# Output-projection weights emitted with the last score row, their low parts on VectorE, a new PSUM pool order, and a closing addition on two engines

## The chip, the core and the metric

The kernel runs on one core of one Trainium2 chip. The metric is the device time of one execution in microseconds (us). Five engines work side by side, each through its own list of instructions in a fixed order: TensorE (PE: matmuls, with its weight loads shown as PEld), VectorE (DVE), ScalarE (ACT), GpSimd (POOL) and SyncE (SP), which here only issues DMA transfers. An engine whose next instruction must wait holds back all that is queued behind it.

## The reference

One encoder layer on x of 1024 frames by 1024 features, in float32:

```python
u = rms_norm(h, mix_norm_gain)
proj = u @ w_in
aq, ak, av, dqkv, dgate, da, db = jnp.split(proj, SPLITS, axis=-1)
...
o_att = rms_norm(chunked_rel_attention(aq, ak, av, ...), att_out_gain)   # 8 heads of 64, band of 9 chunks
...
o_dn = rms_norm(gated_delta_rule(dq, dk, dv, log_decay, beta), dn_out_gain) * silu(dgate)  # 4 heads of 128
mixed = jnp.concatenate([o_att, o_dn], axis=-1) @ w_out
h = h + mixed
z = rms_norm(h, ffn_norm_gain) @ w_ff1
h = h + jnp.square(jax.nn.relu(z)) @ w_ff2
```

## The kernel before

Each product of full precision is made of three matmuls. `split` (L202 to L204) takes a float32 tile apart: ScalarE casts it to a high part `_h` (L203), and another engine subtracts that from the tile to get the low part `_l` (L204). `mm3` (L217 to L223; its matmul is L222) then adds hi·hi, hi·lo and lo·hi into one PSUM bank. A weight block goes through `load_w` (L208): SP issues its load into a raw tile `_r` (L210), of which the pool "wr" has three slots, ScalarE makes the high part, and the low part goes in turn to GpSimd and VectorE (`lo_turn`, L213). A fourth load can be issued only when the first block's low part is done and its slot free.

The program has these stages, in order of time: the input projections; the two mixers, attention and delta rule, woven together (to about 545 us); the output projection with `w_out` (547 to 648); the first feed-forward product `ff1` (649 to 960); the second, `ff2` (to 1266); and the last stores. Both feed-forward products use a scheme of seven block products p1 to p7 (one Strassen-like step), so that additions on VectorE feed TensorE; they keep PSUM tiles of two banks from a pool `psw` of four, tag "bk" (L1327, L1415).

`attention` (L829 to L1184) is a planner. It keeps a model clock, and in each turn emits the cheapest ready step: a score unit, a transpose ("flip"), a product with the values, a delta-rule step, and, once all flips are out and the delta rule has come to its last steps (L1124), a step of the generator `outputs()`, which is `out_proj` (L1186). What is emitted early gets an early place in the engines' lists, which a scheduler then settles by its own estimates.

`out_proj` computes, transposed, 512 columns by 512 frames at a time: `weights(0)` loads the eight 128x512 blocks of the first column half of `w_out` in the order 4, 5, 6, 7, 0, 1, 2, 3; `mixed(0)` splits the mixers' results for the first 512 frames (`mh`, `ml`; blocks 4 to 7 are the delta rule's, tile `mixd`, 0 to 3 attention's, tile `mixa`); `rows(0, 0)` makes four PSUM banks `op` of 24 matmuls each; then `weights(1)`, `rows(1, 0)`, `mixed(1)`, `rows(1, 1)`, `rows(0, 1)`. After each bank VectorE adds the residual x (`h`, L1223). Names used below: `wo_k_r`, `wo_k_h`, `wo_k_l` are the raw, high and low tiles of block k of `w_out`. `c_att`, `c_po`, `c_o` belong to the last delta-rule step, `t_tpa`, `t_tpb`, `t_ta`, `t_tb`, `t_on`, `t_o` to the last attention tile (transposes on TensorE, copies out of PSUM, the product with the values). `wa` are the first weights of `ff1` (L1315), two loads of 512 KB. On GpSimd the rsqrt chains of the normalisations run (`t_v`, `c_v`, L187 to L199).

PSUM has eight banks. The mixers' pools take them in the order of their allocation: `ps_a` three (L132), `ps_t` two, `ps_o` one, `ps_d` two. The banks `op` come from `ps_a`. `ff1`'s first tile of two banks lies where the mixers' first two banks lay.

At the end of `ff2`, with kb the last, partial sums y1 to y7 are merged and stored: `merge(nc.gpsimd, 5, 7)` (L1558) adds y7 to y5 in two halves of 128x1024 on GpSimd, whose stores ScalarE's queue issues (L1464); product p4 is then subtracted from y4 in four quarters on VectorE (L1566), each stored by SP (L1567).

Of the kernel before, what the change touches and what calls it, by code (L numbers as in the profile page):

```python
# [11 lines left out]
ALU = mybir.AluOpType  # L12
AX = mybir.AxisListType

P = 128
SEQ = 1024
DM = 1024
NKT = DM // P
# [25 lines left out]
NV = 6  # L44
# [54 lines left out]
def hymba_kernel(  # L99
# [20 lines left out]
    nc = tc.nc  # L120
    PS = bass.MemoryType.PSUM
# [4 lines left out]
    mixer = ctx.enter_context(ExitStack())  # L126
# [2 lines left out]
    pools = {tag: mixer.enter_context(tc.tile_pool(name="pool_" + tag, bufs=n)) for tag, n in slots.items()}  # L129
    spool = mixer.enter_context(tc.tile_pool(name="spool", bufs=12))  # L130
    mpool = mixer.enter_context(tc.tile_pool(name="mpool", bufs=1))
    ps_a = mixer.enter_context(tc.tile_pool(name="ps_a", bufs=3, space=PS))  # L132
    ps_t = mixer.enter_context(tc.tile_pool(name="ps_t", bufs=2, space=PS))
    ps_o = mixer.enter_context(tc.tile_pool(name="ps_o", bufs=1, space=PS))
    ps_d = mixer.enter_context(tc.tile_pool(name="ps_d", bufs=2, space=PS))

    def page(tag, name, dt=F32, w=512):
        return pools[tag].tile([P, w], dt, tag=tag, name=name, bufs=slots[tag])
# [8 lines left out]
    def part(t, i):  # L147
        return t[:, i * 512:(i + 1) * 512]
# [53 lines left out]
    def split(src, hi, lo, hi_eng, lo_eng):  # L202
        a = nc.scalar.copy(hi, src) if hi_eng is nc.scalar else hi_eng.tensor_copy(hi, src)  # L203
        return a.ins, lo_eng.tensor_tensor(lo, src, hi.bitcast(F32), ALU.subtract).ins  # L204

    lo_turn = [0]

    def load_w(src, name, tags=("wh", "wl")):  # L208
        raw = page("wr", name + "_r")
        nc.sync.dma_start(out=raw, in_=src)  # L210
        hi = page(tags[0], name + "_h", F32R)
        lo = page(tags[1], name + "_l", F32R)
        lo_turn[0] += 1  # L213
        split(raw, hi, lo, nc.scalar, nc.gpsimd if lo_turn[0] % 2 else nc.vector)
        return hi, lo

    def mm3(ps, terms, first=True, last=True):  # L217
        n = 3 * len(terms)
        i = 0
        for (ah, al), (bh, bl) in terms:  # L220
# [8 lines left out]
    u = [[(page("u", f"uh{hf}_{k}", F32R), part(u_low[k // 4], k % 4) if hf else page("u", f"ul{hf}_{k}", F32R))  # L229
          for k in range(NKT)] for hf in range(2)]  # L230
# [580 lines left out]
    def delta_all(ab, kTs, W):  # L811

        Ys, D = {}, {}
        yield dict(M=chained(delta_merge(0, W, Ys), delta_merge(1, W, Ys)))
        for c in range(NT + LATE):
            gens = {}
            if c < NT:
                gens["S"] = delta_state(c, ab, kTs, Ys, D)
            if 0 < c <= NT:
                gens["O"] = delta_out(c - 1, ab, kTs, D)  # L820
            if c + 2 < NT:
                gens["M"] = delta_merge(c + 2, W, Ys)
                if c == 2:
                    gens["M"] = chained(delta_low(1, W, "wh"), gens["M"])
            if c >= LATE:
                gens["F"] = delta_fin(c - LATE, D)
            yield gens

    def attention(after, delta, values, outputs):  # L829


        def bias_page(tag, name):
# [239 lines left out]
        units = [(g, t, pp) for g in range(2) for t in range(NT) for pp in range(2)]  # L1072
        size = [min(t + 1, 5) for g, t, pp in units]
        total, spent, deltas, begun, multiplied = sum(size), 0, 0, 0, 0
# [22 lines left out]
        while True:  # L1097
# [36 lines left out]
            k = best[2]  # L1134
            if k in live:
                gen = live[k][0]
                before = clock.now
                want = next(gen, None)
                deltas += clock.now - before
                if want is None:  # L1140
                    del live[k]
                else:
                    live[k] = gen, want
            elif k == "multiply":
                multiply(*units[multiplied][0:2])
                pe(2 * 218 * size[multiplied] + 300)
                spent += 2 * size[multiplied]
                t = give("o", on("s", 366, clock.now + LATENCY, ahead=True))
                later.append((t, finish, units[multiplied][0:2]))
                multiplied += 2  # L1150
            elif k == "later":
                _, step, args = later.pop(0)
                step(*args)
                if step is finish:
                    t = give("t", on("v", 420, pe(220), ahead=True))
                    if args[0]:
                        t = on("v", 853, on("g", 3200, on("s", 780, t)))
                        later.append((t + MARGIN, turn, args[1:]))
                        later.sort(key=lambda p: p[0])
                else:  # L1160
                    give("t", on("v", 682, pe(440), ahead=True))
            elif k == "flip":
                want = next(flipping[0], None)
                flipping = want and (flipping[0], want)
                if want is None:
                    flipped += 1
            elif k == "score":
                g, t, pp = units[begun]
                score(g, t, pp)
                begun += 1  # L1170
                if pp and begun + 2 < len(units):
                    start(*units[begun + 2][0:2])
                if pp and not g:
                    load_rest(t + 1)
            elif k == "values":
                if next(values, None) is None:
                    values_left = False
                else:
                    give("a", on("s", 690, pe(5500)))
            else:  # L1180
                next(outputs_gen)
                pe(690)
                fill += 1
        return outputs_gen or outputs()  # L1184

    def out_proj(result):  # L1186


        order = (4, 5, 6, 7, 0, 1, 2, 3)
        w, parts, R, begun = [], [], {}, []  # L1190

        def weights(j):
            w.append([None] * NKT)
            for k in order:
                w[j][k] = load_w(w_out[k * P:(k + 1) * P, j * 512:(j + 1) * 512], f"wo{j}_{k}",
                                 (("wh", "u"), ("u", "wl"))[j])

        def mixed(hf):
            parts.append([None] * NKT)
# [33 lines left out]
                nc.scalar.mul(part(r, i), part(r, i), fgain[:, 4 * j + i:4 * j + i + 1])  # L1233
            return acc

        weights(0)
        mixed(0)
        acc = yield from rows(0, 0, None)
        weights(1)
        acc = yield from rows(1, 0, acc)  # L1240
        nc.sync.dma_start(out=sq_dr[:, 0:TH], in_=acc)
        mixed(1)
# [172 lines left out]
    def ff2(psw, pools):  # L1415

        NK = 4
        y = {i: quarter(f"y{i}") for i in (1, 2, 3, 4, 5, 6)}
# [5 lines left out]
        y = {i: [wide(t, 0), wide(t, 1)] for i, t in y.items()}  # L1424
# [43 lines left out]
        for kb in range(nb):  # L1468
# [40 lines left out]
            def merge(eng, i, z):  # L1509
                for m in range(2):  # L1510
                    eng.tensor_tensor(y[i][m], y[i][m], y[z][m], ALU.add)  # L1511
# [43 lines left out]
            if last:  # L1555
                merge(nc.vector, 7, 6)
                merge(nc.vector, 4, 7)
                merge(nc.gpsimd, 5, 7)  # L1558
                store(y[5], 1, 1, nc.scalar)
            ps = product(f"p4{kb}", prep4, last)  # L1560
            if not last:
# [31 lines left out]
    kT = []  # L1593
# [8 lines left out]
    for _ in delta_proj(u, DK, 4, "dk", None, kT, w_dk, first):  # L1602
        pass
    ab = ab_proj(u)
    W, result = [], {}
    after = []
    values = att_proj(u, AV, "v", after)
    interleave(
# [1 line left out]
                 att_proj(u, AK, "k"), att_proj(u, AQ, "q"), first_steps(values, NV)), 1.0),  # L1610
        (chained(delta_prep(kT, ab), (1000 for _ in delta_low(0, W, "pp"))), 0.35))
    clock.reset()
    rest = attention(after[NV - 1], delta_all(ab, kT, W), values, lambda: out_proj(result))
    for _ in rest or ():
        pass
    mixer.close()
# [50 lines left out]
```

## Time and profile before

| what | before |
|---|---|
| time, median of 3 runs | 1276.42 us (1275.62 to 1279.3) |
| the profiled execution's own time | 1273.11 us |
| its span | 1271.0 us |
| mean granted TensorE clock | 0.995 |
| PE busy / PEld busy | 1241.2 us (98%) / 1033.3 us (81%) |
| DVE busy / ACT busy / POOL busy | 926.5 (73%) / 547.6 (43%) / 289.8 us (23%) |

The profile is one execution; its own time is 2.1 us above its span, and lies 3.3 us below the median of the runs. In a row of a timeline stand the start, the duration, the engine, the line, what is written from what, how many instructions ("x3"), and in brackets how long the engine stood idle before them and on what it waited. In a row of the windows each engine's busy time in that stretch is followed by its number of instructions; the figures at the end are the granted TensorE clock (1.00 is full speed), the mean busy share of the DMA engines and GB/s.

### The profile page before, as it was taken

The numbers are of one execution on the slowest core, as the hardware profiler recorded it, in microseconds if no ns is written. First come the engines' busy times: TensorE is split into PE (matmuls) and PEld (weight loads), VectorE is DVE, ScalarE is ACT, GpSimd is POOL, SyncE is SP. The second block draws the span as 40 slices with busy tenths as digits, with TensorE's granted clock in tenths as the row PEclk, the third lists the DMA queues.
The fourth block names the chain that finished last, engine by engine and source line by source line (L and its number), as shares of the span: only waits on it lengthen the run. The fifth ranks groups of instructions, "written<-read, shape, count | busy, mean of one in ns | idle before, by whom it ended". The sixth has DMA issues, their size and how long they took to land.

```text
span 1271.0 us, 18018 instructions
## 1 busy us (share of the span) xinstructions
PE 1241.2 (98%) x6686; PEld 1033.3 (81%) x6686; DVE 926.5 (73%) x1388; ACT 547.6 (43%) x899; POOL 289.8 (23%) x487
## 2 busy tenths in 40 slices
PE   9999999999998999889999999999999999999998
PEld 8778878778888898778878788888887888888886
DVE  7899987654236577774349777677669997997988
ACT  7323132232245665654445454544445543333331
POOL 4425461344132345543210000000000000000034
PEclk9999999999999999989999999999999999999999
DMA  7214353564585532134441333332259623332002
GB/s 226 67 42 139 101 157 107 121 162 118 175 245 150 162 109 71 40 109 133 141 141 67 116 133 117 132 100 96 86 199 368 211 83 112 121 100 94 7 34 99
DMA packets 135398, 158.53 MB, mean 125 GB/s; under 512 B 31760, under 2 KB 79376, under 8 KB 134800
## 3 DMA queue, kind: packets, MB, share of 16 engines
q1 hardware_dynamic: 117216, 135.11, 35.0%
q10 hardware_dynamic: 18096, 22.29, 5.2%
q8 instruction: 52, 0.85, 0.3%
q14 instruction: 34, 0.28, 0.1%
HBM read 109.91 MB, written 47.45 MB: 124 GB/s over the span
## 4 chain that ended last, share of the span: by engine, by line
PE 51%; DVE 8%; issue 2%; ACT 1%; POOLq 1%; POOL 0%; DVEq 0%; ACTq 0%
PE p L1439 21%; PE q L1343 20%; PE op L222 6%; PE t_o L1024 1%; POOLq L1662 1%; DVE ml L204 1%; DVE h L1285 1%; DVE y L1511 0%; PE t_sa L925 0%; DVE q_0a_l L204 0%; DVE y L1507 0%; PE t_tpb L985 0%; DVE p43b_l L204 0%; DVE p73b_l L204 0%; DVE p43a_l L204 0%
## 5 line engine op out<-in xcount | busy, mean ns | idle before, releaser
L1511 POOL TENSOR_TENSOR y<-y,y 128x1024 f32<-128x1024 f32 x6 | 19.3, 3242 | 590.5 <-DVE y L1507 571.6
L1507 DVE TENSOR_TENSOR y<-y,p 128x1024 f32<-128x1024 f32 x46 | 55.1, 1216 | 5.4 <-PE p L1439 4.5
L222 PE MATMUL op<-mh,wo_l 128*128 128x512 f32 x128 | 50.1, 399 | 1.1 <-POOL wo_l L204 1.1
L222 PE MATMUL op<-mh,wo_h 128*128 128x512 f32 x128 | 50.6, 398 | 0.1
L222 PE MATMUL op<-ml,wo_h 128*128 128x512 f32 x128 | 50.2, 395 | 0.0
L945 DVE CUSTOM_DVE_ANT_0 t_pb<-t_sb,biasn 128x256 f32<-128x256 f32 (+1 forms) x64 | 23.2, 401 | 29.8 <-PE t_sb L925 29.8
L964 ACT ACTIVATE t_pb<-t_pb,t_nm 128x256 f32<-128x256 f32 (+1 forms) x64 | 31.4, 491 | 18.1 <-DVE t_nm L956 16.7
L1223 DVE TENSOR_TENSOR h<-op,op_x 128x512 f32<-128x512 f32 x16 | 10.8, 687 | 28.8 <-PE op L222 28.8
L1230 POOL TENSOR_TENSOR op_q<-op_q 128x512 f32<-128x512 f32 x14 | 19.6, 1397 | 47.3 <-ACT op_q L1229 47.2
L222 PEld LDWEIGHTS op<-mh,wo_l 128*128 128x128 f32 x128 | 24.4, 191 | 6.9 <-POOL wo_l L204 1.5
L222 PEld LDWEIGHTS op<-mh,wo_h 128*128 128x128 f32 x128 | 24.4, 191 | 5.9 <-issue 0.5
L222 PEld LDWEIGHTS op<-ml,wo_h 128*128 128x128 f32 x128 | 24.4, 190 | 5.2
L956 DVE CUSTOM_DVE_ANT_0 t_pa<-t_sa,biaso,t_nm 128x384 f32<-128x384 f32 (+2 forms) x48 | 25.0, 543 | 2.3 <-PE t_sa L925 2.0
L222 PE MATMUL g_ps<-uh,wg_h 128*128 128x512 f32 x64 | 25.3, 396 | 1.2 <-ACT wg_h L203 1.2
L968 ACT ACTIVATE t_pa<-t_pa,t_nm 128x384 f32<-128x384 f32 (+2 forms) x48 | 26.4, 550 | 0.0
L222 PE MATMUL aq_ps<-waq_h,uh 128*128 128x512 f32 x64 | 25.4, 400 | 0.8 <-ACT waq_h L203 0.8
L925 PE MATMUL t_sb<-ks,t_q 128*128 128x256 f32 (+1 forms) x144 | 24.0, 294 | 1.7 <-DVE t_nm L945 1.3
L222 PE MATMUL g_ps<-uh,wg_l 128*128 128x512 f32 x64 | 25.2, 393 | 0.4 <-POOL wg_l L204 0.4
L222 PE MATMUL dq_ps<-uh,wdq_h 128*128 128x512 f32 x64 | 25.5, 398 | 0.0
L222 PE MATMUL dv_ps<-uh,wdv_l 128*128 128x512 f32 x64 | 25.4, 397 | 0.0
L222 PE MATMUL dq_ps<-ul,wdq_h 128*128 128x512 f32 x64 | 25.3, 395 | 0.0
L222 PE MATMUL av_ps<-wav_l,uh 128*128 128x512 f32 x64 | 25.2, 394 | 0.0
(1109 smaller groups left out, 4306.7 us busy)
## 6 DMA issues: line engine op xcount, KB each, us to landing
wa<-in_w_ff_dram SPq DMA_DIRECT2D x32, 512.0 KB
a<-in_w_ff_dram SPq DMA_DIRECT2D x32, 512.0 KB
b<-f_dr SPq DMA_DIRECT2D x32, 512.0 KB
f_dr<-yy ACTq DMA_DIRECT2D x16, 512.0 KB
t_q<-q_dr SPq DMA_DIRECT2D x30, 256.0 KB
f_dr<-zz ACTq DMA_DIRECT2D x13, 512.0 KB
ks<-k_dr SPq DMA_DIRECT2D x16, 256.0 KB
wo_r<-in_w_out_dram SPq DMA_DIRECT2D x16, 256.0 KB
```

The source lines that it names most:

```text
L204: return a.ins, lo_eng.tensor_tensor(lo, src, hi.bitcast(F32), ALU.subtract).ins
L222: nc.tensor.matmul(ps, a, b, start=(first and i == 0), stop=(last and i == n - 1))
L925: nc.tensor.matmul(o, q[m][:, i * P:(i + 1) * P], k[:, c], start=(m == 0), stop=(m == 1))
L945: nc.vector.tensor_tensor_reduce(sb[:, c], bk[:, c], new[g][pp][:, c], -1.0, 3.0e38, ALU.add, ALU.min, nm[:, 4 + i:5 + i])
L956: nc.vector.tensor_tensor_reduce(sa[e][:, 0:wa], bk[:, 0:wa], old[g][i][:, 384 - wa:384], -1.0, nm[:, 4 + i:5 + i], ALU.add, ALU.min, nm[: ...
L964: nc.scalar.activation(sb[:, c], sb[:, c], AF.Exp, bias=m, scale=-1.0, accum_out=T["sums"][:, 4 + i:5 + i])
L968: nc.scalar.activation(sa[e][:, 0:wa], sa[e][:, 0:wa], AF.Exp, bias=m, scale=-1.0, accum_out=T["sums"][:, i:i + 1])
L1230: nc.gpsimd.tensor_tensor(acc, acc, sq, ALU.add)
L1343: nc.tensor.matmul(part(ps, q), l[:, s], r, start=(k + m == 0), stop=(k == 3 and m == 2))
L1439: nc.tensor.matmul(part(ps[q], 0) if by_rows else part(ps[q // 2], q % 2), l[:, s], part(r, k), start=(i + k + m == 0), stop=(i + k + m == 4))
L1507: nc.vector.tensor_tensor(y[i][m], y[i][m], ps[m], op)
L1511: eng.tensor_tensor(y[i][m], y[i][m], y[z][m], ALU.add)
```

## The change

Four things are changed.

1. `weights(0)` becomes `out_weights(w, 0)` and is no longer the first thing in `out_proj`: the planner emits it, at high priority, as soon as it has emitted the last score unit. `out_weights(w, 1)` stays between `rows(0, 0)` and `rows(1, 0)`.
2. The low parts of all sixteen blocks of `w_out` go to VectorE; half of them were on GpSimd.
3. `ps_a` is allocated last of the mixers' PSUM pools, so its three banks are the last three, and the first two belong to `ps_t`.
4. The closing y5 += y7 is shared: its first half stays on GpSimd, its second goes to VectorE.

```diff
-    ps_a = mixer.enter_context(tc.tile_pool(name="ps_a", bufs=3, space=PS))
     ps_t = mixer.enter_context(tc.tile_pool(name="ps_t", bufs=2, space=PS))
     ps_o = mixer.enter_context(tc.tile_pool(name="ps_o", bufs=1, space=PS))
     ps_d = mixer.enter_context(tc.tile_pool(name="ps_d", bufs=2, space=PS))
+    ps_a = mixer.enter_context(tc.tile_pool(name="ps_a", bufs=3, space=PS))
...
-    def load_w(src, name, tags=("wh", "wl")):
+    def load_w(src, name, tags=("wh", "wl"), low=None):
...
-        split(raw, hi, lo, nc.scalar, nc.gpsimd if lo_turn[0] % 2 else nc.vector)
+        split(raw, hi, lo, nc.scalar, low or (nc.gpsimd if lo_turn[0] % 2 else nc.vector))
...
-    def attention(after, delta, values, outputs):
+    def attention(after, delta, values, weights, outputs):
...
                 begun += 1
+                if begun == len(units):
+                    with tc.high_priority():
+                        weights()
...
-    def out_proj(result):
...
+    def out_weights(w, j):
+        w.append([None] * NKT)
+        for k in order:
+            w[j][k] = load_w(w_out[k * P:(k + 1) * P, j * 512:(j + 1) * 512], f"wo{j}_{k}",
+                             (("wh", "u"), ("u", "wl"))[j], nc.vector)
...
-        weights(0)
         mixed(0)
         acc = yield from rows(0, 0, None)
-        weights(1)
+        out_weights(w, 1)
...
-                merge(nc.gpsimd, 5, 7)
+                for m, eng in enumerate((nc.gpsimd, nc.vector)):
+                    eng.tensor_tensor(y[5][m], y[5][m], y[7][m], ALU.add)
```

**VectorE where the output projection begins.** These rows follow the last score's maximum (L956) on VectorE, first before the change.

```order
L807 SCALAR_TENSOR_TENSOR mixd_6009<-c_tpo,dng,c_jg 128x4x128
L780 TENSOR_TENSOR c_att<-c_mt,c_Lt 128x512
L1051 TENSOR_TENSOR t_on<-t_on,t_tot 128x256
L204 TENSOR_TENSOR ml_6651<-mixd_4680,mh_6650 128x512
L786 TENSOR_TENSOR c_o<-c_o,c_po 128x512
L204 TENSOR_TENSOR ml_6655<-mixd_4680,mh_6654 128x512
```

The same place after the change:

```order
L204 TENSOR_TENSOR wo_4_l<-wo_4_r,wo_4_h 128x512
L204 TENSOR_TENSOR wo_5_l<-wo_5_r,wo_5_h 128x512
L204 TENSOR_TENSOR wo_6_l<-wo_6_r,wo_6_h 128x512
L807 SCALAR_TENSOR_TENSOR mixd_6009<-c_tpo,dng,c_jg 128x4x128
L780 TENSOR_TENSOR c_att<-c_mt,c_Lt 128x512
L1051 TENSOR_TENSOR t_on<-t_on,t_tot 128x256
L204 TENSOR_TENSOR ml_6651<-mixd_4680,mh_6650 128x512
```

Three low parts stand ahead of `c_att`; before, `wo_5_l` stood fifteen rows further down, and `wo_4_l` and `wo_6_l` were on GpSimd, behind both rsqrt chains and between `c_v` and `c_y`.

**ScalarE at the same place**, from the last exponential of the scores (L968) on, before the change:

```order
L968 ACTIVATE t_pa_6422,t_sum<-t_pa_6422,t_nm 128x384
L203 CAST mh_6650<-mixd_4680 128x512
L203 CAST mh_6654<-mixd_4680 128x512
L1006 COPY t_ta_6519<-t_tpa_6515 128x384
L203 CAST mh_6666<-mixa_5563 128x512
L203 CAST mh_6670<-mixa_5563 128x512
L203 CAST mh_6658<-mixd_4680 128x512
L1056 ACTIVATE t_on,t_oss<-t_on 128x512
L203 CAST mh_6662<-mixd_4680 128x512
```

And after the change:

```order
L968 ACTIVATE t_pa_6422,t_sum<-t_pa_6422,t_nm 128x384
L203 CAST mh_6650<-mixd_4680 128x512
L203 CAST mh_6654<-mixd_4680 128x512
L203 CAST mh_6658<-mixd_4680 128x512
L1056 ACTIVATE t_on,t_oss<-t_on 128x512
L203 CAST wo_7_h<-wo_7_r 128x512
L203 CAST mh_6662<-mixd_4680 128x512
L203 CAST wo_0_h<-wo_0_r 128x512
L203 CAST wo_1_h<-wo_1_r 128x512
L541 ACTIVATE c_po<-c_o 128x512
L203 CAST wo_2_h<-wo_2_r 128x512
L203 CAST wo_3_h<-wo_3_r 128x512
```

The five casts of the blocks that are loaded late, `wo_7_h` to `wo_3_h`, moved up from behind the attention tile's last copy; that tile's copy `t_ta` (L1006) now follows `wo_3_h`, and the casts of `mixa` follow the copies.

**VectorE at the end of the program**, before the change:

```order
L1511 TENSOR_TENSOR y_9457<-y_9457,y_0_9460 128x1024
L1511 TENSOR_TENSOR y_9457<-y_9457,y_1_9461 128x1024
L1566 TENSOR_TENSOR y_9457<-y_9457,p_11528 128x512
L1566 TENSOR_TENSOR y_9457<-y_9457,p_11529 128x512
L1566 TENSOR_TENSOR y_9457<-y_9457,p_11530 128x512
L1566 TENSOR_TENSOR y_9457<-y_9457,p_11531 128x512
```

And after it (lines below the added ones are four or five higher):

```order
L1514 TENSOR_TENSOR y_9457<-y_9457,y_0_9460 128x1024
L1514 TENSOR_TENSOR y_9457<-y_9457,y_1_9461 128x1024
L1562 TENSOR_TENSOR y_9458<-y_9458,y_1_9461 128x1024
L1570 TENSOR_TENSOR y_9457<-y_9457,p_11528 128x512
L1570 TENSOR_TENSOR y_9457<-y_9457,p_11529 128x512
L1570 TENSOR_TENSOR y_9457<-y_9457,p_11530 128x512
L1570 TENSOR_TENSOR y_9457<-y_9457,p_11531 128x512
```

The shared addition's second half (L1562) stands ahead of the four subtractions (L1570) that free the last stores.

On SP the three loads `wo_4_r`, `wo_5_r` and `wo_6_r`, which stood behind the delta rule's loads `l_w` (L630) and `m_sa` (L665), now stand among the `l_w` loads, 7, 7 and 2 rows earlier; the other five stand where they stood, right behind the two loads `wa`.

More of the change, by code (lines that the diff above doesn't have):

```diff
@@ L1184, in attention, with out_proj @@
         return outputs_gen or outputs()
-    def out_proj(result):
[L1189 to L1196, printed above, removed]
+    order = (4, 5, 6, 7, 0, 1, 2, 3)
+    def out_weights(w, j):
[3 more added lines that the diff above has]
+                             (("wh", "u"), ("u", "wl"))[j], nc.vector)
+    def out_proj(result, w):
+        parts, R, begun = [], {}, []
         def mixed(hf):
@@ L1604, in hymba_kernel @@
     ab = ab_proj(u)
-    W, result = [], {}
+    W, w_o, result = [], [], {}
     after = []
@@ L1612, in hymba_kernel @@
     clock.reset()
-    rest = attention(after[NV - 1], delta_all(ab, kT, W), values, lambda: out_proj(result))
+    rest = attention(after[NV - 1], delta_all(ab, kT, W), values,
+                     lambda: out_weights(w_o, 0), lambda: out_proj(result, w_o))
     for _ in rest or ():
```

## The prediction

> **What bounds the kernel now.** I read the page first: the span, the busy line, and the chain that ended last.
>
> ```profile
> span 1271.0 us, 18018 instructions
> PE 1241.2 (98%) x6686; PEld 1033.3 (81%) x6686; DVE 926.5 (73%) x1388; ACT 547.6 (43%) x899; POOL 289.8 (23%) x487
> PE 51%; DVE 8%; issue 2%; ACT 1%; POOLq 1%; POOL 0%; DVEq 0%; ACTq 0%
> ```
>
> PE is busy in all but 30 us of the span, so time can only come out of PE's idle spots, or out of busy time that is stretched. Where those are, the table of windows tells.
>
> ```profile
> 545.00:555.00 10.00, 6.68 (x39) 4.88 (x37) 8.62 (x18) 7.98 (x19) 4.29 (x9) 0.85 0.30 103
> 555.00:560.00 5.00, 4.44 (x21) 3.42 (x23) 2.35 (x3) 1.24 (x2) 4.59 (x8) 0.62 0.51 157
> 560.00:575.00 15.00, 15.00 (x95) 12.44 (x92) 7.03 (x9) 5.10 (x10) 5.40 (x10) 1.00 0.39 123
> 600.00:648.00 48.00, 47.70 (x208) 38.56 (x206) 17.36 (x21) 15.84 (x23) 12.93 (x9) 1.00 0.31 104
> 660.00:720.00 60.00, 59.00 (x276) 48.77 (x275) 57.85 (x52) 33.51 (x33) 0.00 (x0) 1.00 0.27 89
> ```
>
> The first figure behind the length is PE. At 545 to 560, where the mixers give way to the output projection, PE is idle for 3.9 us of 15, and the granted clock falls to 0.62; from 560 on PE is full again. At 660 to 720 VectorE is as full as PE (57.85 of 60). PE's timeline at the hole:
>
> ```profile
> 546.08 1.16 PE L516 MATMUL c_po<-c_vn,c_att 128*128 128x128 f32 x8 [0.24 <-DVE c_att L780]
> 547.00 0.94 PE L222 MATMUL op<-mh,wo_h 128*128 128x512 f32 x3
> ...
> 549.74 0.66 PE L985 MATMUL t_tpb<-ident,t_pb 128*128 128x128 f32 x4 [0.78 <-ACT t_on L1056]
> 551.15 0.55 PE L1001 MATMUL t_tpa<-ident,t_pa 128*128 128x128 f32 x3 [0.76 <-ACT t_ta L1006]
> 552.66 0.90 PE L1001 MATMUL t_tpa<-ident,t_pa 128*128 128x128 f32 x3 [0.97 <-ACT t_tb L991]
> ...
> 555.56 0.80 PE L222 MATMUL op<-mh,wo_l 128*128 128x512 f32 x1 [1.14 <-POOL wo_l L204]
> ...
> 557.86 0.63 PE L222 MATMUL op<-ml,wo_h 128*128 128x512 f32 x1
> 558.29 0.63 PE L222 MATMUL op<-mh,wo_l 128*128 128x512 f32 x1
> ...
> 559.32 0.88 PE L1024 MATMUL t_o<-t_ta,vt 128*64 128x128 f32 x12
> ...
> 647.22 0.39 PE L222 MATMUL op<-ml,wo_h 128*128 128x512 f32 x1
> 647.45 0.39 PE L222 MATMUL op<-mh,wo_l 128*128 128x512 f32 x1
> 648.71 0.47 PE L1343 MATMUL q<-b11h,q_0a_h 128*128 128x512 f32 x1 [0.88 <-DVE h L1223]
> ```
>
> PE has output-projection matmuls to do, but after six of them the list needs a low part; meanwhile it steps through the attention tile's transposes, each waiting for a copy. Starts of successive `op` matmuls lie 0.43 us apart at 558 and 0.23 at 647: the first run at half clock. [...]
>
> The four helpers at the place:
>
> ```profile
> 545.34 0.69 DVE L780 TENSOR_TENSOR c_att<-c_mt,c_Lt 128x512 f32<-128x512 f32 x1
> ...
> 553.92 3.28 POOL L204 TENSOR_TENSOR wo_l<-wo_r,wo_h 128x512 fp32r<-128x512 f32 x2
> ...
> 546.00 1.13 ACT L203 CAST mh<-mixd 128x512 fp32r<-128x512 f32 x2
> 558.12 0.62 ACT L203 CAST wo_h<-wo_r 128x512 fp32r<-128x512 f32 x1 [5.14 <-DMA wo_r<-in_w_out_dram]
> ...
> 543.56 0.94 SPq L1315 DMA_DIRECT2D wa<-in_w_ff_dram  x2
> 555.54 6.13 SPq L210 DMA_DIRECT2D wo_r<-in_w_out_dram  x5
> ...
> L204 POOL TENSOR_TENSOR wo_l<-wo_r,wo_h x8: 1280/1290/1724, 553.9 to 592.2; 128x512 fp32r<-128x512 f32 x8
> L204 DVE TENSOR_TENSOR wo_l<-wo_r,wo_h x8: 679/693/1372, 554.8 to 592.7; 128x512 fp32r<-128x512 f32 x8
> ```
>
> GpSimd starts `wo_4_l` only at 553.92, behind its rsqrt chains. SP's remaining five loads go out at 555.54, when that low part has freed a raw slot; the first lands 2.6 us later, at 558.12.
>
> **Part 1 and 2, early weights and low parts on VectorE.** From the end of the transposes before `c_po` (545.84: 546.08 less the 0.24 idle) to 559.32 PE takes 13.48 us. Its work there at full clock, by the spacing of the same instructions where the clock is 1.00: `c_po` 0.9, fifteen `op` matmuls at 0.227 make 3.4, four groups of transposes, `t_tpa` three times 0.33 and `t_tpb` 0.44, make 1.4, `t_tpo` 0.44: 6.2 us in all. So 7.3 us are lost, by waiting and half clock together.
>
> After the change VectorE makes `wo_4_l`, `wo_5_l` and `wo_6_l` at about 544.4 to 546.2 (three at 0.61, the issue distance in a row of such operations, ahead of its other work), since their high parts are old. This costs `c_att` 1.5 to 1.9 us: it ends at about 547.6 and not 546.0. PE meanwhile has three `op` matmuls whose `mh` is cast at 546.0 to 546.6, waits about 0.8 us for that, 0.3 for `c_att`, and 0.1 for the first `ml`. Then its list holds only `op` matmuls of blocks 4 to 7 for three banks, 36 of them or 8.2 us, in which the other operands arrive. That is 1.2 us of waiting where 7.3 were lost, and too little in any stretch to lower the clock: a gain of 6.1 if all that follows is on time.
>
> What follows: `wo_7`, `wo_0` and `wo_1` are issued when the three low parts free their slots, at 545.2 to 546.6, but the 1 MB of `wa`, issued at 543.56, is ahead of them on the DMA engines. At the 370 to 390 GB/s that transfers reach (the last row quoted under part 4), I put their landing at 549.3 to 550.7 (2.6 us alone, as above, plus about 1.5). `wo_2` and `wo_3` each need one more turn (low part on VectorE, issue, 2.6 us), and land at about 553.7 and 554.6. ScalarE's list holds `t_ta`, then the casts of `mixa`, behind `wo_3_h`. So `t_ta` is done at 555.6 to 556.5, where PE wants its bank back at about 556.5, and the first `mixa` block is ready at 557.7 where PE wants it at 558.0. Both joints fit, with 0.0 to 0.9 us to spare; by estimate I take off 0.5 for them. On GpSimd the rsqrt chains gain 1.3 to 3.3 us by the missing low parts. In the second column half nothing is gained or lost: VectorE takes four more low parts, 2.8 us, in stretches where it is busy 7.03 of 15. PE is full at 560 to 575 and 600 to 648, so the gain is carried to the end of the stage. **Term: +5.6 us, bounds +2.5 and +7.0.**
>
> Upstream, three loads of 256 KB move ahead on SP by 2 to 7 places near 372 to 382 us. They take SP 0.6 us apiece, and the same number of transfers stands ahead of the loads that PE waits for there in both orders. I take nothing, bounds -1 and +0.5; the price if that fails is a rival below.
>
> **Part 3, PSUM order.** The wait of 0.88 us at 648.71 is for VectorE's `h`, which frees the last `op` bank: `ff1`'s first tile lies on it. With `ps_a` last, that tile lies on banks of `ps_t`, which the output projection doesn't use, and the tile that lies on the last `op` bank is the third. PE starts 0.88 us earlier. What follows is the stretch in which VectorE is full; its chain starts from a ScalarE cast that waits for PE's first product, so it moves along. **Term: +0.8, bounds 0 and 0.9.**
>
> **Part 4, the closing addition.**
>
> ```profile
> 1258.02 4.62 DVE L1511 TENSOR_TENSOR y<-y,y 128x1024 f32<-128x1024 f32 x4
> 1262.56 1.87 DVE L1566 TENSOR_TENSOR y<-y,p 128x512 f32<-128x512 f32 x3
> 1265.88 0.69 DVE L1566 TENSOR_TENSOR y<-y,p 128x512 f32<-128x512 f32 x1 [1.44 <-PE p L1439]
> 1259.38 7.84 POOL L1511 TENSOR_TENSOR y<-y,y 128x1024 f32<-128x1024 f32 x2 [13.70 <-DVE y L1511]
> L1511 POOL TENSOR_TENSOR y<-y,y x6: 2348/2894/5522, 1222.4 to 1264.9; 128x1024 f32<-128x1024 f32 x6
> 1264.93 2.70 ACTq L1464 DMA_DIRECT2D out_dram<-y  x2
> 1263.27 3.66 SPq L1567 DMA_DIRECT2D out_dram<-y  x4
> GB/s 0 174 369 369 374 389 389 394 164 0 0 0 0 0 0 0 0 0 0 0 0 0 67 374 405 384 343 394 374 394 379 379 369 384 384 394 220 0 0 0
> ```
>
> The last row is 1255 to 1271 in slices of 0.4 us. GpSimd's first half took 5.52 us, nearly all of VectorE's adds long (to 1262.56) plus a further 2.35, which is what the second took when VectorE had little to do. [...]
>
> By rows alone: VectorE's new add, 1.15 us (4.62 by 4), stands ahead of the three subtractions, so the first store leaves at 1264.4, not 1263.27. It does not delay the fourth, which waits for PE in 1.44 us of idle time. The 2 MB of closing stores run without a gap at 370 to 390 GB/s from 1264.1 on, and need 5.5 us: the end is set by when they begin. So the end moves out by 0.9 (1.15, less what the fuller queue gains). The other bound: if only the last ScalarE store, issued at 1267.2, sets the end, it can leave 1.3 earlier. **Term: -0.9, bounds -1.2 and +1.3.**
>
> **Sum.** 5.6 + 0.8 - 0.9 = 5.5 us. The profiled execution, 1273.11, would be at 1267.6; the median of the runs, 1276.42, at **1270.9**. Bounds added: 2.5 + 0 - 1.2 - 1 = 0.3, and 7.0 + 0.9 + 1.3 + 0.5 = 9.7; not all fall one way, and the forecast's own range is 1267.2 to 1273.0.
>
> **The rivals.**
>
> *ScalarE takes over as the waited-for.* The late blocks are cast ahead of `t_ta` and `mixa`. If `wo_7` lands at 552 (the 1 MB of `wa` wholly ahead, and each turn 3.2 us and not 2.6), `wo_3_h` ends near 558.5, PE waits about 2.5 us at the attention tile, and the clock may fall again as at 555 to 560 (0.62 of 5 us, 1.9 lost). For it: two joints without slack. Against: PE has 8.2 us of `op` work ahead. Gain left: 5.6 - 4.4 = 1.2, total 1.2 + 0.8 - 0.9 = 1.1, time 1275.3. Chance 0.20.
>
> *`ff1` swallows part.* VectorE is full to 720; what PE gains ahead of it is worth only what moves the VectorE chain. If none of the 0.88 us arrives and the weights' transfers hold 1 us more, total 3.7, time 1272.7; against it, that chain hangs on PE's first product. Chance 0.12.
>
> *Slower: SP held by the early loads.*
>
> ```profile
> 404.55 1.44 PE L640 MATMUL l_p<-l_w,l_xa 32*32 32x32 f32 x32 [3.63 <-issue]
> 388.68 0.85 SPq L210 DMA_DIRECT2D wo_r<-in_w_out_dram  x2
> ```
>
> PE stands 3.63 us for the delta rule's small loads, which SP issues one after the other. `wo_5_r` and `wo_6_r` now come ahead of more of them, and wait for raw slots whose former users are late casts of attention. Each us that SP stands there is a us of PE. It decides from 5.5 us of standing; at 9.5 the time is 1280.4, slower by 4. Against: the slots' users had run at 371 and 377, when SP comes to the loads. Chance 0.05.
>
> *The change does not do what it says:* the low parts stand early in the list, but a semaphore shared with a late instruction holds them. Then the first low part comes no earlier than 553 and the time is 1276. Chance 0.04.
>
> **How the numbers follow.** The forecast has 0.59, the rivals 0.20, 0.12, 0.05 and 0.04. A measurement of this kernel can tell 0.3%, 3.8 us, from no change: below 1272.6 is faster, above 1280.2 slower. Faster: of the forecast 0.57 (its range ends 0.4 beyond the bound), of the second rival 0.07, which lies on it, and of the first 0.06, where its price is under the 5.5 - 3.8 = 1.7 us that the forecast has to spare: 0.70. Slower: 0.05. Same: the 0.25 left. The range takes in the forecast and most of the first rival: 1267.2 to 1275.6.
>
> **What would show it.** Right: in the windows 545 to 560 PE busy near 14 of 15 at clock 1.00; no idle on `wo_l`; SP's five `wo_r` at 545 to 553; `ff1`'s first matmul directly behind the last `op`, near 642.2; first closing store 1.1 us later against the last p4 matmul. Wrong: idle of over 1.5 us before `t_tpa`, `t_tpb` or the `mixa` blocks on ScalarE; a clock under 1.00 at 545 to 565; `l_p`'s wait over 3.6 us.

## The result, and the profile after

| what | before | after |
|---|---|---|
| time, median | 1276.42 us (1272.14 to 1279.41, 5 runs) | 1266.8 us (1264.75 to 1267.93, 5 runs) |
| ratio of the times | | 0.9921, 95% interval 0.9898 to 0.9944 |
| the profiled execution's own time, span | 1273.11, 1271.0 us | 1267.93, 1266.0 us |
| its mean granted clock | 0.995 | 0.996 |

The change makes the kernel faster by 9.6 us by the medians, 10.1 by the ratio (7.1 to 13.0). The prediction, 1270.9 with a range from 1267.2 on, was too high, and the measured time lies just outside the range. The two profiled executions differ by 5.2 us only, which is close to the 5.5 of the sum: the profile and the median do not tell the same. Why is the main question of what follows.

The page after the change, span and busy times:

```profile
span 1266.0 us, 18010 instructions
PE 1240.5 (98%) x6686; PEld 1032.9 (82%) x6686; DVE 932.1 (74%) x1397; ACT 547.0 (43%) x899; POOL 277.5 (22%) x478
```

The table of windows after the change, the hole (545 to 560) between two stretches in which the granted clock is not 1.00:

```profile
390.00:395.00 5.00, 4.80 (x33) 4.36 (x35) 3.18 (x13) 1.68 (x5) 0.20 (x1) 0.70 0.84 226
395.00:400.00 5.00, 5.00 (x47) 4.66 (x44) 1.97 (x8) 2.65 (x7) 2.89 (x7) 0.96 0.48 138
...
545.00:550.00 5.00, 4.97 (x26) 4.06 (x27) 3.59 (x7) 2.34 (x6) 2.12 (x6) 1.00 0.75 266
550.00:555.00 5.00, 4.97 (x22) 3.75 (x20) 4.34 (x9) 2.91 (x7) 1.14 (x3) 1.00 0.43 141
555.00:560.00 5.00, 4.17 (x24) 3.35 (x24) 3.61 (x6) 4.11 (x9) 2.34 (x6) 1.00 0.39 123
...
965.00:970.00 5.00, 5.00 (x17) 3.95 (x16) 3.54 (x4) 1.91 (x3) 0.00 (x0) 0.66 1.03 408
```

At 545 to 560 TensorE is busy 14.1 of 15 us (11.1 before) at full clock. But there is half clock after 390 and after 965 (0.50 in windows of 1 us, 392 to 395 and 966 to 968). By the rows 0.30 and 0.04 of two windows of 5 us are missing, and 0.34 of one: two stretches of 3.4 us each, which cost up to 1.7 apiece. The profile of before had none at 965. TensorE's timeline, with its waits:

```profile
390.20 1.08 PE L925 MATMUL t_sb<-ks,t_q 128*128 128x128 f32 x8 [1.95 <-DMA t_q<-q_dr]
...
404.18 1.19 PE L640 MATMUL l_p<-l_w,l_xa 32*32 32x32 f32 x32
...
542.61 1.06 PE L516 MATMUL c_mt<-c_jq,kT 128*128 128x128 f32 x8
...
545.02 0.96 PE L222 MATMUL op<-mh,wo_h 128*128 128x512 f32 x3 [0.81 <-ACT mh L203]
...
555.83 0.66 PE L985 MATMUL t_tpb<-ident,t_pb 128*128 128x128 f32 x4 [0.86 <-ACT t_ta L1006]
...
640.66 0.40 PE L222 MATMUL op<-mh,wo_l 128*128 128x512 f32 x1
640.89 0.39 PE L1346 MATMUL q<-b11h,q_0a_h 128*128 128x512 f32 x1
```

Two waits are left in the hole, 0.81 for `mh` and 0.86 for the copy `t_ta`; `ff1` starts 0.23 us behind the last `op`, which is the distance of two matmuls. The wait of 3.63 us at `l_p` is gone too, though a wait for `t_q` at 390 stands at 1.95 (0.42 in the profile of before). The helpers at the hole:

```profile
543.48 8.89 SPq L210 DMA_DIRECT2D wo_r<-in_w_out_dram  x5
...
545.18 0.68 DVE L780 TENSOR_TENSOR c_att<-c_mt,c_Lt 128x512 f32<-128x512 f32 x1
...
549.39 0.62 ACT L203 CAST wo_h<-wo_r 128x512 fp32r<-128x512 f32 x1 [2.20 <-DMA wo_r<-in_w_out_dram]
...
554.78 0.62 ACT L203 CAST wo_h<-wo_r 128x512 fp32r<-128x512 f32 x1 [0.73 <-DMA wo_r<-in_w_out_dram]
555.31 0.85 ACT L1006 COPY t_ta<-t_tpa 128x384 f32<-128x384 f32 x2
```

SP's five loads now start at 543.48 (555.54 before). The first is cast at 549.39 and the last at 554.78, and `t_ta` follows it at 555.31: the joint that the prediction called tight is late by 0.86. The end of the program:

```profile
1251.77 4.62 DVE L1514 TENSOR_TENSOR y<-y,y 128x1024 f32<-128x1024 f32 x4
1256.31 1.21 DVE L1562 TENSOR_TENSOR y<-y,y 128x1024 f32<-128x1024 f32 x1
1257.45 1.87 DVE L1570 TENSOR_TENSOR y<-y,p 128x512 f32<-128x512 f32 x3
1259.63 0.69 DVE L1570 TENSOR_TENSOR y<-y,p 128x512 f32<-128x512 f32 x1 [0.31 <-PE p L1442]
1253.13 6.66 POOL L1562 TENSOR_TENSOR y<-y,y 128x1024 f32<-128x1024 f32 x1 [13.70 <-DVE y L1514]
1258.15 2.53 SPq L1571 DMA_DIRECT2D out_dram<-y  x4
```

GpSimd's half took 6.66 us (5.52 before): it ends 2.3 us, the time of one such addition (2.35 before), after VectorE's row of adds is through (1257.45), and that row is now one longer. From TensorE's last product to the end of the span it is 6.8 us (5.55 before).

The change of 5.0 us between the two spans is put together as follows, by the start of the same instruction in both. The last matmul of the mixers' last step `c_mt`, 0.78 behind the start of its row: 545.02 and 543.39, 1.63 earlier. From there to `ff1`'s first matmul: 103.69 and 97.50, 6.19 less. From that to the last product: 616.74 and 618.31, 1.57 more, the half clock at 965. From there to the end: 1.25 more. That these 5.0 us come so near the 5.5 of the sum is in part luck: 1.63 that the sum had at nothing and 1.57 of half clock nearly cancel.

### The profile page after: what moved, and what is told of

Same layout as the page of the kernel before. It is cut to its first block, busy times and chain, and to the rows that moved or that the text cites. A ratio compares the mean times of both kernels' runs of the same rounds, so it can differ in the third digit from the quotient of the medians.

```text
span 1266.0 us, 18010 instructions
## 1 busy us (share of the span) xinstructions
PE 1240.5 (98%) x6686; PEld 1032.9 (82%) x6686; DVE 932.1 (74%) x1397; ACT 547.0 (43%) x899; POOL 277.5 (22%) x478
## 4 chain that ended last, share of the span: by engine, by line
PE 54%; DVE 6%; ACT 1%; issue 1%; DMA 1%; POOL 0%; DVEq 0%; ACTq 0%; SPq 0%
PE p L1442 23%; PE q L1346 20%; PE op L222 6%; PE t_o L1024 1%; DMA wo_r<-in_w_out_dram 1%; DVE h L1288 1%; PE t_sa L925 0%; DVE q_0a_l L204 0%; PE t_tpb L985 0%; PE t_sb L925 0%; PE c_pv L516 0%; PE t_tpa L1001 0%; PE t_tpo L520 0%; PE c_pq L516 0%; DVE t_pa L956 0%
## 5 line engine op out<-in xcount | busy, mean ns | idle before, releaser
L1514 POOL TENSOR_TENSOR y<-y,y 128x1024 f32<-128x1024 f32 x4 | 11.5, 2895 | 577.3 <-DVE y L1510 572.2
L1227 DVE TENSOR_TENSOR h<-op,op_x 128x512 f32<-128x512 f32 x16 | 10.8, 687 | 28.2 <-PE op L222 28.2
L956 DVE CUSTOM_DVE_ANT_0 t_pa<-t_sa,biaso,t_nm 128x384 f32<-128x384 f32 (+2 forms) x48 | 24.9, 543 | 2.3 <-PE t_sa L925 2.0
L968 ACT ACTIVATE t_pa<-t_pa,t_nm 128x384 f32<-128x384 f32 (+2 forms) x48 | 26.4, 550 | 0.0
```

The lines of the kernel that those rows point to most:

```text
L956: nc.vector.tensor_tensor_reduce(sa[e][:, 0:wa], bk[:, 0:wa], old[g][i][:, 384 - wa:384], -1.0, nm[:, 4 + i:5 + i], ALU.add, ALU.min, nm[: ...
L968: nc.scalar.activation(sa[e][:, 0:wa], sa[e][:, 0:wa], AF.Exp, bias=m, scale=-1.0, accum_out=T["sums"][:, i:i + 1])
```

## The experiments

Times stand against runs of the kernel before on the same chip: 1276.15 (29 runs), 1275.67 (23 runs) and 1276.62 us (23 runs) for runs 1 to 4, 5 to 8 and 9 to 12. "Less" and "more" without a further word are the ratio's share of that median; where two runs with edits are compared, it is by their medians. "c_mt" is the start of that last matmul, "the stretch" goes from there to `ff1`'s first matmul.

**1. The kernel before, once more**, unchanged.

> The kernel before, unchanged, profiled once more. Theory (the clock's drops vary): TensorE's idle spots lie where they did, within 0.3 us, but the stretches at half clock do not: one to four stretches of about 3.4 us, at other places than 405 and 552 to 559; each execution's time follows its mean granted clock, about 1.3 us for each 0.001, and the five times spread over 4 us or more around 1276. Rival (the profile of before was no odd one; the surplus gain is work removed): half clock at the same two places again, times within 0.2% of each other at one clock.

Measured: 1275.1 us (1270.61 to 1278.23, 12 runs), ratio 0.9982 (0.9965 to 1.0), so two sets of runs of one kernel may lie 0.2% apart. Its profiled execution took 1276.61 us. The stretches at half clock in that profile:

```profile
405.00:410.00 5.00, 5.00 (x65) 4.73 (x63) 1.12 (x4) 2.14 (x7) 0.00 (x0) 0.66 0.85 224
...
555.00:560.00 5.00, 3.49 (x8) 2.82 (x9) 2.98 (x6) 0.62 (x1) 4.76 (x6) 0.53 0.42 147
560.00:565.00 5.00, 5.00 (x48) 3.96 (x47) 2.65 (x3) 2.59 (x5) 3.28 (x5) 0.79 0.45 142
975.00:980.00 5.00, 5.00 (x17) 3.93 (x16) 3.53 (x4) 2.15 (x3) 0.00 (x0) 0.66 1.03 408
```

The first profile of before had one stretch at 405 and two at 552 to 559; here the waits at the same places (2.62 us at `l_p`; 0.78, 0.76, 0.97 and 1.60 in the hole) are followed by half clock again, and the wait of 1.8 us in `ff2` by one more. So the places are those that the rival named, with one added, and the theory was wrong about them. About the times it was right: over 87 runs of this kernel the time goes with the mean granted clock of the run.

| mean granted clock | runs | mean time, us |
|---|---|---|
| 0.990 | 6 | 1280.0 |
| 0.991 | 15 | 1279.0 |
| 0.992 | 11 | 1277.1 |
| 0.993 | 1 | 1276.6 |
| 0.994 | 25 | 1275.5 |
| 0.995 | 22 | 1273.2 |
| 0.996 | 6 | 1271.6 |
| 0.997 | 1 | 1271.3 |

0.001 of the clock goes with 1.4 us; it would be 1.27 (0.001 of the span) if half clock were the whole of the difference. Runs of one clock still lie up to 6 us apart (0.994: 1272.2 to 1278.2), so it is not all. The mean over the 87 is 1275.7 us at 0.9934; the profiled execution of before, at 0.995, was one of the better ones. The eleven timed runs of the changed kernel have 1266.4 us at 0.9972.

**2. Parts 1 and 2 alone.** The diff is that of the change without the pool order and without the closing addition.

> Parts 1 and 2 alone (early weights, all low parts on VectorE). Theory: the idle time at 545 to 560 goes, as in the full change; the PSUM wait of 0.88 us stays, the closing stores are as before. Against before: 9 us less (the full change's measured 9.6 less 0.8 for the PSUM order plus about 1 for the closing addition), 1267. Rival (another part brings the surplus): 5.6 us less, 1271.

Measured: 1265.04 us (6 runs), ratio 0.9915 (0.9895 to 0.9935), 10.8 less. The first two parts carry the whole gain, as the theory had it, and a little more than expected. This profiled execution (1264.36 us) has no half clock at any of the places:

```profile
390.00:395.00 5.00, 4.98 (x52) 4.55 (x52) 3.35 (x13) 2.27 (x8) 0.30 (x2) 1.00 0.89 234
550.00:555.00 5.00, 4.49 (x24) 3.41 (x22) 3.15 (x7) 2.68 (x7) 2.86 (x6) 1.00 0.61 204
965.00:970.00 5.00, 5.00 (x23) 4.12 (x23) 3.46 (x4) 2.65 (x3) 0.00 (x0) 1.00 1.03 410
```

**3. Part 3 alone**, the pool order.

> Part 3 alone. Theory: the wait of 0.88 us before the first matmul of the first feed-forward product goes, all else as before: 0.8 us less, about 1275.6, less than the times differ from one another. Rival (the PSUM order also helps the mixers or the feed-forward stage): 4 us less, 1272.5.

Measured: 1275.62 us (12 runs), ratio 0.9999 (0.9982 to 1.0015). In the profile `ff1` starts 0.23 us behind the last `op` (1.26 before), so the wait of 1.03 is gone; the times cannot show so little, and rule out the rival's 4 us.

**4. Part 4 alone**, the closing addition.

> Part 4 alone. Theory: the first closing store leaves 1.1 us later against TensorE's last product, so 0.9 to 1.2 us more, 1277.5, below what the times can tell; in the profile the second half of the addition runs on VectorE ahead of the subtractions, and GpSimd's half takes longer than its 5.5 us. Rival (the sharing helps): the last store is issued 1.3 us earlier and the time falls by 1.3.

Measured: 1277.53 us (12 runs), ratio 1.0006 (0.9988 to 1.0024): not to be told by the times. GpSimd's half in the profile:

```profile
1260.92 6.67 POOL L1559 TENSOR_TENSOR y<-y,y 128x1024 f32<-128x1024 f32 x1 [13.70 <-DVE y L1511]
```

From the last product to the end it is 6.81 us, and 5.54 in run 1: 1.3 us more, as expected. VectorE's half, 1.22 us at 1264.10, falls inside GpSimd's, which is longer by about as much (1.15 over the 5.52 of before): the sharing gained nothing.

**5. Part 1 alone**, low parts in turn on GpSimd and VectorE (`nc.vector` left out of `out_weights`).

> Part 1 alone: the weights emitted with the last score, low parts in turn on GpSimd and VectorE as before. GpSimd's first two low parts now stand ahead of its rsqrt chains. Theory (the place in the lists, not the engine, closes the hole): the hole at 545 to 560 is gone but for 1 to 2 us, no half clock there, 1267 (8 to 9.5 less than before). Rival (VectorE is what makes the low parts timely): half of it, 1271 to 1272.

Measured: 1267.28 us (6 runs), ratio 0.9941 (0.9922 to 0.996), 7.5 less. GpSimd makes `wo_4_l` and `wo_6_l` at 540.04, long ahead of need. The theory's 8 to 9.5 was a little too much, and the rival's half too little. The hole closes without VectorE's help, with no half clock in it (1.00 from 545 to 560); there is one wait more:

```profile
544.42 1.16 PE L516 MATMUL c_po<-c_vn,c_att 128*128 128x128 f32 x8 [1.56 <-DVE c_att L780]
```

So the place in the lists counts most. The engine is worth 1.4 us by the stretch (99.5 us, 98.1 in run 2) and 3.3 by the ratios, whose intervals overlap a little.

**6. The full change without high priority.** On SP the three early loads stand where they stood before; VectorE's rows at 545 are those of the full change.

```diff
-                    with tc.high_priority():
-                        weights()
+                    weights()
```

> The full change, but the weights are emitted with the last score without high priority: the three early loads stand on SP where they stood before, VectorE's list at 545 is as in the full change. It separates the hole at 545 from the order of SP's loads at 372 to 390. Theory (the hole is all that counts): as the full change within 1.5 us, 1266.8. Rival (the loads' new order also takes away part of the wait of 3.6 us for the delta rule's loads and its half clock): 2 to 4 us more than the full change, 1269 to 1271.

Measured: 1268.97 us (12 runs), ratio 0.9956 (0.9939 to 0.9973), 2.2 more than the full change; by the ratios it would be 3.8 to 4.5 more (the full change has 0.9921, and 0.9926 in run 11), and the intervals just overlap. The rival was right: the order of the loads is worth something. In this profile TensorE's wait for `l_p` is back, with c_mt at 547.08, while the stretch is 97.31 us, like that of the full change:

```profile
406.60 1.17 PE L640 MATMUL l_p<-l_w,l_xa 32*32 32x32 f32 x32 [3.52 <-issue]
```

**7. The full change without part 4.**

> The full change without part 4 (the closing addition stays on GpSimd). Theory: the closing stores begin 1.1 us earlier against TensorE's last product, 1 us less than the full change: 1265.7 at the full change's 1266.8. Rival: no difference, or 1 us more.

Measured: 1265.47 us (6 runs), ratio 0.9919 (0.9897 to 0.9942): 1.3 less than the full change, as expected, though within the intervals (by the ratios it is 0.3 to 0.9). From the last product to the end it is 5.73 us again.

**8. The hole filled with idle work**, in the kernel before.

```diff
-    def mm3(ps, terms, first=True, last=True):
+    def mm3(ps, terms, first=True, last=True, idle=0):
...
                 i += 1
+                if i == 2:
+                    for _ in range(idle):
+                        nc.tensor.matmul(ps[0:64, :], zero, bh, start=False, stop=False)
```

> The kernel before, with 18 matmuls more in the hole: zero weights, 64 columns by 512, added into the three open output-projection banks, so the result is the same and TensorE has 4.1 us more to do (18 at 0.227) where it used to wait. The scheduler also sets the attention tile's product ahead of the first low part. Theory (half clock, not the waits alone, is a large part of the loss): clock 1.00 at 545 to 560, and in spite of the added work 2 to 5 us less than before, 1271 to 1274. Rival (the waits are all): no half clock is saved, and the time is as before or up to 4 us more.

Measured: 1274.37 us (12 runs), ratio 0.9992 (0.9975 to 1.0009). The clock in the profile is 1.00 from 545 to 565, and the mean clock over the runs rose from 0.9934 to 0.996. TensorE did 4.1 us more, and the kernel was no slower: the stretch is 104.16 us, where it is 103.4 to 104.6 in profiles of before and of runs 1, 4 and 9, whose hole is open. But the 2 to 5 us expected didn't show in the times. The place of the low parts was unchanged, and the rearranged rows brought a new wait of 1.71 us for a `wo_h` at 592. Up to that wait the run was ahead, 4.1 us of added work and all: its 121st `op` product starts 40.28 us behind c_mt, where it is 41.62 to 42.89 in the four profiles just named. So in the hole full clock, together with the rearranged rows, was worth 1.3 to 2.6 us beyond the idle time that was filled, and the new wait took that back. Which part of it was clock alone this run doesn't say.

**9. The three early loads alone.** The kernel before, with the loads of blocks 4, 5 and 6 issued where the full change has them, and the splits where they were.

```diff
+                if begun == len(units):
+                    with tc.high_priority():
+                        for k in (4, 5, 6):
+                            raws[k] = page("wr", f"wo0_{k}_r")
+                            nc.sync.dma_start(out=raws[k], in_=w_out[k * P:(k + 1) * P, 0:512])
```

> The kernel before, with only the three early loads (blocks 4, 5 and 6 of the first column half) put where the full change has them on SP; high and low parts, GpSimd, VectorE and the hole at 545 as before. Theory (the order of SP's loads at 372 to 390 is worth something by itself): TensorE's step c_mt near the end of the mixers starts about 2 us earlier than in the kernel before, the hole is unchanged, 1273.5 to 1274.5. Rival (the upstream order is worth nothing, what the profiles show there is chance): 1276 and c_mt where it was.

Measured: 1273.17 us (12 runs), ratio 0.9983 (0.9966 to 0.9999), 2.2 less (0.1 to 4.3), c_mt at 544.07 (545.02 before, 545.97 in run 1). The hole is open (4.4 us idle from 543 to 560). As the theory had it, though the interval all but reaches no change. In the traces the three loads stand 20, 17 and 7 transfers earlier on SP than before, not 7, 7 and 2: they are issued at 372.65, 377.93 and 384.58 in the full change, at 386.60, 388.68 and 389.15 before. What SP waits for at 388 to 405, in the kernel before:

```profile
SPq L634 <- DMA t_q<-q_dr: 0.9, 1, 0.9
SPq L700 <- PE c_po L516: 0.8, 1, 0.8
SPq L703 <- DMA wo_r<-in_w_out_dram: 0.7, 1, 0.7
SPq L633 <- DMA t_q<-q_dr: 0.6, 1, 0.6
SPq L905 <- PE t_tpa L1001: 0.5, 1, 0.5
```

And in run 9, the whole list:

```profile
SPq L701 <- PE t_tpb L986: 0.5, 1, 0.5
```

Before the change SP stands three times, 2.2 us, among the small loads `l_xa` for earlier transfers, once for a weight load and twice for `t_q`. From the first `l_xa` to the last it takes 11.7 to 13.0 us to issue in the seven profiles with the old order (before and runs 1, 3, 4, 6, 8 and 10), and 10.7 in the seven others. TensorE's wait at `l_p` is for the last of them, as far as the profiles tell: `l_p` starts 0.8 to 1.0 us behind the start of the last issue in each of the seven profiles in which it waits.

The wait is 1.7 to 3.6 us in six of the seven profiles with the old order; in run 3 there is none, since there TensorE itself comes late, after a stretch at half clock at 392 (0.71 at 390 to 395). In the seven others it is none, or 0.26 us (run 2). The new order has its price too: the wait for `t_q` near 390 is 0.3 to 2.1 us with the old order (mean 1.3) and 1.4 to 2.6 in the others (1.9). Taken together, c_mt lies at 544.1 to 547.1 with the old order (mean 545.5) and at 541.9 to 545.1 in the others (543.0): 2.4 us earlier, near the 2.2 of the times.

**10. Part 2 alone**, all low parts on VectorE at their old place.

> Part 2 alone: all low parts on VectorE, emitted where they were. They then stand behind VectorE's work for the attention tile, at about 554.5 in the timeline of before, not ahead of c_att. Theory (the place in the lists closes the hole): the hole stays, 0 to 1.5 us less than before, 1274.5 to 1276. Rival (freeing GpSimd's chain is what helps): 3 us less or better.

Measured: 1273.94 us (12 runs), ratio 0.9985 (0.9967 to 1.0003), 1.9 less (4.2 less to 0.4 more). Between the theory and the rival, nearer to the theory. The three low parts are made at 554.07, and the hole stays:

```profile
550.00:555.00 5.00, 3.10 (x18) 2.33 (x20) 5.00 (x12) 2.23 (x5) 4.07 (x9) 0.65 0.00 0
```

**11. The full change once more.**

> The full change, profiled and timed once more, to see which of its idle spots let the clock fall. Theory: 1266.8 within 1 us; no half clock at 545 to 560; half clock, if any, after the waits at 390 to 410 or at 965. Rival: half clock at 545 to 560 in this execution.

Measured: 1266.68 us (6 runs), ratio 0.9926 (0.9902 to 0.9951). The clock in this profile:

```profile
390.00:395.00 5.00, 5.00 (x41) 4.36 (x39) 4.11 (x18) 1.20 (x4) 0.88 (x3) 0.66 0.87 243
550.00:555.00 5.00, 4.55 (x23) 3.49 (x22) 3.71 (x8) 2.80 (x7) 2.36 (x5) 1.00 0.62 174
555.00:560.00 5.00, 5.00 (x28) 3.96 (x26) 3.94 (x6) 2.84 (x6) 1.23 (x4) 1.00 0.26 88
965.00:970.00 5.00, 5.00 (x18) 3.99 (x18) 3.48 (x4) 2.95 (x3) 0.00 (x0) 0.74 1.02 408
```

Half clock after the waits at 390 and in `ff2`, none in the hole, as the theory had it. The stretch is 97.03 us.

**12. The change without part 4, and the three early loads later**, behind attention's last bias loads (`behind` collects those loads' instructions).

```diff
-                    with tc.high_priority():
+                    with tc.issue_after(behind[-1]), tc.high_priority():
                         weights()
```

> The change without part 4, and with the three early loads queued on SP behind the last of attention's bias loads, so that no weight load stands ahead of the small loads of the delta rule at 372 to 405. Theory (SP is the bound at 384 to 405, each weight load there costs about 0.6 us of issue): the wait at l_p shrinks by 1 to 2 us and with it the chance of half clock, 1.5 to 3 us less than without part 4 alone: 1262.5 to 1264. Rival (the wait is for the transfers, not for SP): 1265.5 as without part 4.

Measured: 1263.1 us (1260.69 to 1266.15, 6 runs), ratio 0.9904 (0.9878 to 0.9929), the least of all, 2.4 below run 7. SP waits for no transfer among the small loads, TensorE does not wait at `l_p`, and `t_q` is late by 1.40 us only (2.57 in run 7), though half clock follows that wait too (0.66 at 390 to 395):

```profile
388.84 1.08 PE L926 MATMUL t_sb<-ks,t_q 128*128 128x128 f32 x8 [1.40 <-DMA t_q<-q_dr]
```

It beats both kernels by the medians; against the full change and run 7 the intervals overlap. The theory had a wait at `l_p` shrink, but run 7's profile has none to shrink; a gain over run 7 would have to come from the wait for `t_q` and from half clock, and is not shown.

## Why the prediction was wrong, and where it was right

**The step that failed first: "I take nothing, bounds -1 and +0.5"** for the three loads that move on SP. They are worth about 2.2 us: run 9, which has only them, is 2.2 less (0.1 to 4.3), run 6, which lacks only them, 2.2 more, and c_mt comes 2.4 earlier in the mean of seven profiles against seven. The prediction took the loads to move by 2 to 7 places, where they move by 7 to 20 transfers. It counted the issues, found the same number ahead of the loads that TensorE waits for, and stopped there. What it should have read is SP's own list of waits: in the trace of before SP stands for transfers to land, 2.2 us in three places, in the middle of the loads whose lateness it had quoted as a wait of 3.63 us. Two of the weight loads stood just ahead of them, with only two loads of `t_q` between. That these weight loads are what made the `t_q` transfers land late is a reading of the order, not shown by itself.

**The step that failed second: carrying the difference of two profiled executions over to the medians.** The sum was made against 1273.11 and then taken off 1276.42, as if the 3.3 us between them would stay. They don't. 0.7 of them is that the median of the five runs lies above the mean of 87 (1275.7). Of the other 2.6, 2.0 go with the clock: the mean over the 87 runs is 0.9934, in the profile it is 0.995, and 0.001 of the span is 1.27 us. The changed kernel's profiled execution, at 0.996, lay on the other side, 1.5 us above the mean of eleven runs (1266.4 at 0.9972). So 4.1 of the 9.3 us between the means of both kernels are not in the two profiles.

By estimate, half clock makes 0.0066 x 1274 - 0.0028 x 1264 = 4.9 of the 9.3. This is rough: the mean clock also counts half clock behind the last product, where it costs nothing (1.1 us lost in the profile of before, 1.8 in that of after), and half clock that falls into waits. The change takes away the largest idle spot and, in most profiles, the one at `l_p`, and its runs lie closer together (1263.86 to 1267.93 over eleven, against 1269.52 to 1281.57 over 87; standard deviations 1.2 and 2.8). That half clock costs time, and does not only go with it, is shown at one place: from `ff1`'s first matmul to the last product the six profiles with a stretch of it take 1.6 us more than the eight without, with the same work and the same waits. That it makes up the rest of the difference is argued; run 8 raised the clock and was no faster, if with 4.1 us more to do.

**Parts 1 and 2 in the hole: right, though the loads came late.** 5.6 and 0.8 together were forecast for the stretch; it shrank by 6.2 in the first pair of profiles, and by 6.8 between the means of four profiles with the hole open (before, runs 1, 4 and 9: 104.0) and two of the full change (97.3). Of this 1.03 is the PSUM order, so the hole gave 5.2 to 5.8 for 5.6. TensorE's waits came nearly as worked out: 0.81 for `mh` (0.8), none for `c_att` beyond that (0.3), and 0.86 at the tight joint, for which 0.5 was taken off. The loads did not come as worked out. The forecast's times are those of the profile of before, in which the last `c_mt` lies 1.63 us later; counted so, the first late block is cast at 551.0, where its landing was put at 549.3, and the last at 556.4 and not at 554.6. The first took 5.9 us from its issue to its cast, for which 4.1 was reckoned. That is part of the way to the first rival, and TensorE's other work covered most of it. Full clock from 545 to 560: right, 1.00 in all three windows after the change and in runs 2, 5, 11 and 12. That half clock goes with the waits, and that the short ones left over do not lower the clock, as the 5.6 takes for granted, no run shows in general: here waits of 0.81 and 0.86 us left the clock at 1.00, and in run 12 one of 1.39 did, but one of 1.40 near 390 in the same run was followed by half clock. That the engine matters less than the place (runs 5 and 10) was not worked out.

**Part 3: right**, 1.03 by the profile for 0.8. **Part 4: right in sign and mechanism**, 1.25 to 1.3 for 0.9: the whole of VectorE's add (1.15) is lost and 0.1 more, and the fuller queue gains nothing. GpSimd's half grew from 5.52 to 6.66 us (6.67 in run 4), by one VectorE add; why it does so no run shows.

**The rivals.** ScalarE as the waited-for came to 0.86 us, not 2.5, and was followed by no half clock (1.00 at 555 to 560); the loads did not hold SP among the small loads, they released it; the low parts were not held back, the first is made at 542.71; `ff1` passed the gain on whole (from its first matmul to the last product 616.7 us in before and in runs 3, 4, 6, 7, 8 and 12, 616.8 in run 2; the other profiles, 1.6 us longer, have half clock there).

What stays open: the terms add up to 2.2 + 6.8 - 1.3 = 7.7 us, the first by the times and the others by the profiles, and the medians say 9.6. The rest of about 2 us may be half clock in executions without a profile, at the wait for `l_p` and in the hole; the clocks of the runs agree with it, and run 4's profile, at 0.993, has 10.2 us of half clock after `l_p` (0.83, 0.50 and 0.65 in the three windows of 5 us from 400 on), but no profile of an execution at 0.990 was had.

## What to carry to other kernels

Before taking a profiled execution's time as the base, look at the mean granted clock of all runs: where the time goes with it (here 1.4 us for 0.001 of it), one profile is a draw from a spread (here 12 us over 87 runs), and a change that removes idle spots can gain more or less than two profiles show (here 9.6 us by the medians, 5.2 by the profiles). A weight load that is far from its use is not free (the place of three of them was worth about 2.2 us here): see what stands behind it on the queue that issues it, and whether that queue waits for transfers to land. Sharing an addition between GpSimd and VectorE gained nothing here: GpSimd's half took 6.66 us where it had taken 5.52, and the end came 1.25 to 1.3 us later.

## What the runs showed of the hardware that was not expected

One wait, at the second half of p5 in `ff2`, measures 1.8 us in before, after and runs 2 and 5 to 12. At that place a stretch of 3.4 us at half clock follows in six of the fourteen profiles (after and runs 1, 5, 9, 10 and 11), and by none in the other eight. Of the eleven waits of 1.4 to 2.6 us for `t_q` near 390, six are followed by such a stretch (after and runs 3, 7, 9, 11 and 12) and five are not (runs 1, 2, 5, 6 and 10). The shortest of the six is 1.40 us (run 12), the longest of the five 2.37 (run 5), so the length of the wait alone does not decide. The stretches themselves measure 3.4 us, or two or three times that: ahead of the last product the fourteen profiles have them of 3.4, 6.8 and 10.2 us.
